# A GpSimd power ahead of all other work, and ten cosine products and eight key sums on VectorE in a hybrid encoder trunk

## The chip, the cores and the metric

The kernel runs on one core of one Trainium2 chip. The metric is the device time of one execution in microseconds (us), the median of several runs. TensorE (PE in the profile) multiplies matrices, VectorE (DVE) and ScalarE (ACT) work element by element, GpSimd (POOL) does a little arithmetic and starts some of the transfers, and SyncE (SP) starts the others.

## The reference

The kernel computes two layers of an encoder on 512 positions of 1024 features. Of each layer this is what matters here:

```python
xn = rms_norm(x, ln1[l])
z = xn @ w_in[l]
a_q, a_i, a_ff, a_fb, a_g, b_u, b_v, c_q, c_k, c_v, gz = split(z)
o_a = hgrn2_bidirectional(a_q, a_i, a_ff, a_fb, lower[l])   # branch A: 4 heads
y_a = rms_norm(o_a, a_norm[l]) * silu(a_g)
y_b = spatial_gating(gelu(b_u), gelu(b_v), w_s[l], b_s[l])  # branch B
qh, kh = partial_rope(c_q, pos), partial_rope(c_k, pos)     # branch C: t1*cos - t2*sin, t2*cos + t1*sin
y_c = window_attention(qh, kh, c_v, sink[l])
merged = (sigmoid(gz_0) * (y_a @ w_br[l, 0]) + sigmoid(gz_1) * (y_b @ w_br[l, 1])
          + sigmoid(gz_2) * (y_c @ w_br[l, 2]))
x = x + merged @ w_out[l]
x = x + square(relu(rms_norm(x, ln2[l]) @ w_up[l])) @ w_down[l]
```

Branch A is a gated linear recurrence in both directions. For one chunk, `attn = einsum(q_t, k_s, exp(b_t - b_s))` over all s up to t. The diagonal of it, where t equals s, has no decay: it is q times the key, and with two directions it is q times the sum of the forward and the backward key.

## The kernel before

**Products.** Every float32 product is three TensorE products of rounded parts: high times high, low times high, high times low (L200 to L202 with positions as the moving side, L242 to L244 for the other orientation). Weights come in pieces of 128x1024 through SP's queue. ACT rounds a piece to its high part `wh` (L195), and DVE subtracts it from the piece to get the low part `wl` (L196).

**Stages of a layer.** First the input is normalized and the wide projections for the values of A, the second half of B and the gates run as seven products instead of eight (L393 to L419 are their sums and products). Then come the branches, described next; then the branch outputs are projected (`yC`, `yA`, with tiles from L242 to L244), turned (`mT`, L1023), put through the output projection `wo`, and then through the MLP. The reciprocal square root of a norm is a power -0.5 on POOL (`rstd_c`, L262; and L818 for branch B). The first of them waits for DVE's L260, and PE's `bc` (L269) spreads its result over the columns.

**Branch A, one head** (`a_head`, L541 on). `ex` holds four rows of running log-decays. Seven levels L = 1, 2, 4 ... 64 follow each other. In each, ACT takes two exponentials of `ex` (`qt`, L552, and `kt`, L555), DVE multiplies `qt` by `q` (L553), PE forms 64-wide blocks `at` (L539), DVE or ACT puts them in place (L543 is the DVE one), and DVE adds across blocks in `ex` for the next level (two L580). At the first level the two keys are also exponentiated into `key` (L560), POOL adds them to `dg` (L562), and PE multiplies the sum by `q` for the diagonal. After the last level, `kd` (ACT, L592) is turned on PE (`kT`, L595), copied by ACT (L597), and multiplied with the values (`stp`, L600), once for each direction. The `q` and `f` of each head are projections of their own; DVE scales them as they leave PSUM (L685 for `q`, L693 for the gate inputs `z` from `f`).

**Branch C.** The key projection `ck` and the four query projections `cq` are rotated by `rot` (L865 to L871): DVE shuffles partitions (L867) and multiplies by the sine (L868), POOL multiplies the unshuffled tile by the cosine (L869), and DVE adds the two (L870). The rotated queries are split into parts (L898 on DVE), and the scores (`sc`, L914 and L915), turned probabilities (`pT`, L943) and outputs (`po`, L948) follow in blocks of 128 positions.

**Order.** The program is written with loops over heads, levels and blocks. A list scheduler with a simulated timeline, with priorities raised or lowered by helpers such as `hp()`, sets the order of the instructions on each engine when the kernel is built. So a change in what one engine is given can move the instructions of all. The order is fixed on each engine at run time, and semaphores tie the engines together. PSUM has eight banks in four pairs, and `q`, `f`, `ck`, `cq` and `gz` share one pair (`m`): a third product in a row waits until DVE or ACT has emptied the first. Tiles of the pool tag `a` (three buffers) hold `qt`, `kt`, `kd`, `qd` and `dg`.

Of the kernel before, what the change touches and what calls it, by code (L numbers as in the profile page):

```python
# [10 lines left out]
ALU = mybir.AluOpType  # L11
# [18 lines left out]
def ap_of(t, off, dims):  # L30
    return bass.AP(tensor=t.tensor, offset=t.offset + off, ap=[t.ap[0]] + dims)
# [28 lines left out]
def trunk(tc, xT, xt, ws, vec, fnb, bsb, snk, wst, rope, cmask, amask, ident, out):  # L60
    nc = tc.nc
# [30 lines left out]
    def nm(s):  # L92
        ctr[0] += 1
        return f"{s}_{ctr[0]}"

    def T(tag, name, dt=F32):
        where = part[HOME[tag]] if tag in HOME else sb
        return where.tile([P, S], dt, tag=tag, bufs=SLOTS[tag], name=nm(name))
# [8 lines left out]
    def Z2(name):  # L107
        return part["br"].tile([P, 2, S], F32, tag="z2", bufs=NZ, name=nm(name))

    def SM(tag, w):  # L110
        return pad.tile([P, w], F32, tag="sm_" + tag, bufs=4 if tag == "lb" else NSM, name=nm(tag))
# [4 lines left out]
    def PT(tag, name):  # L116
        return ps.tile([P, S], F32, tag="p_" + tag, bufs=BANKS[tag], name=nm(name))
# [31 lines left out]
    onep_t = cst.tile([P, 1], F32, name="onep_t")  # L149
    nc.vector.memset(onep_t, 1.0)  # L150

    mhalf_t = cst.tile([P, 4], F32, name="mhalf_t")
    nc.vector.memset(mhalf_t, -0.5)

    pad_t = pad.tile([P, 16], F32, name="pad_t")
    nc.vector.memset(pad_t, 0.0)

    nc.scalar.activation(pad_t[:, 1:2], pad_t[:, 0:1], AF.Square)

    def ln_ap(which, l, kt):  # L160
        c = {"ln1": 0, "ln2": 16, "fn": 32}[which] + (l * 8 if which != "fn" else 0) + kt
        return vec_t[:, c:c + 1]

    def anorm_ap(l):
        return vec_t[:, 40 + l:41 + l]
# [361 lines left out]
    def a_head(l, h, ex, q, vt):  # L527
        H = P // 2
        at = part["br"].tile([P, 4, P], F32, tag="at", bufs=1, name=nm("at"))
        own = part["br"].tile([P, 4, H], F32, tag="own", bufs=1, name=nm("own"))  # L530

        def attn(kk, qq, other=False):

            pt = PT("a", "at")
            for st in range(4):
                for h_ in range(2):
                    k0 = st * P + h_ * H
                    q0 = st * P + (1 - h_ if other else h_) * H
                    nc.tensor.matmul(pt[h_ * H:(h_ + 1) * H, st * H:(st + 1) * H], kk[:, k0:k0 + H], qq[:, q0:q0 + H], start=True, stop=True, skip_group_check=True)  # L539
            return pt[:, 0:4 * H].rearrange("p (a b) -> p a b", a=4)  # L540

        def put(pt, mi):
            nc.vector.copy_predicated(own, ap_of(amask_t, mi * H, [[0, 4], [1, H]]), pt)  # L543

        X, R, Y, PP = 0, S, 2 * S, 3 * S
        for li, L in enumerate(LEVELS):
            nb = 256 // L
            shp = "p (b h i) -> p b h i"
            e_k = ap_of(ex, 0, [[2 * L, nb], [2 * S + L, 2], [1, L]])
            e_q = ap_of(ex, S, [[2 * L, nb], [2 * S + L, 2], [1, L]])  # L550
            qt = T("a", "qt")
            nc.scalar.activation(qt.rearrange(shp, b=nb, h=2), e_q, AF.Exp)  # L552
            nc.vector.tensor_tensor(qt, qt, q, ALU.mult)  # L553
            kt_ = T("a", "kt")
            nc.scalar.activation(kt_.rearrange(shp, b=nb, h=2), e_k, AF.Exp)  # L555
            if L == 1:
                pt = attn(kt_, qt)
                nc.scalar.copy(own, pt)
                key = Z2("key")
                nc.scalar.activation(key, ap_of(ex, 0, [[2 * S, 2], [1, S]]), AF.Exp)  # L560
                dg = T("a", "dg")
                nc.gpsimd.tensor_tensor(dg, key[:, 0], key[:, 1], ALU.add)  # L562
                pt = attn(dg, q)
                put(pt, 0)
            elif L < H:
                put(attn(kt_, qt), li)
            else:
                pt = attn(kt_, qt, True)
                for h_ in range(2):
                    r = slice(h_ * H, (h_ + 1) * H)  # L570
                    nc.scalar.copy(at[r, :, (1 - h_) * H:(2 - h_) * H], pt[r])
                    nc.scalar.copy(at[r, :, h_ * H:(h_ + 1) * H], own[r])

            d = [[2 * L, nb], [1, L]]
            z = [[2 * L, nb], [0, L]]
            for o_, ostep, i_, istep in ((X, PP + L - X, PP + 2 * L - 1, -L), (Y + L, R - Y - L, R, L)):
                o_ap = ap_of(ex, o_, [[ostep, 2]] + d)
                nc.vector.tensor_tensor(o_ap, o_ap, ap_of(ex, i_, [[istep, 2]] + z), ALU.add)  # L580

        W3 = 3 * P
        dec = SM("ms", 4)
        nc.scalar.activation(dec[:, 0:2], ap_of(ex, PP + 2 * P - 1, [[P, 2]]), AF.Exp)
        nc.scalar.activation(dec[:, 2:4], ap_of(ex, R + P, [[P, 2]]), AF.Exp)
        sts, qds = [], []
        for dr, (ko, qo) in enumerate(((0, P), (P, 0))):

            kd = T("a", "kd")[:, 0:W3]
            nc.scalar.activation(kd, ex[:, 2 * dr, ko:ko + W3], AF.Exp)  # L592
            pt = PT("a", "kT")
            for i in range(3):
                nc.tensor.transpose(pt[:, i * P:(i + 1) * P], kd[:, i * P:(i + 1) * P], id_t)  # L595
            kT = part["br"].tile([P, W3], F32, tag="kT", bufs=1, name=nm("kT"))
            nc.scalar.copy(kT, pt[:, 0:W3])  # L597
            ps_ = PT("a", "stp")
            for i in range(3):
                nc.tensor.matmul(ps_[:, i * P:(i + 1) * P], kT[:, i * P:(i + 1) * P], vt[ko // P + i][:, h * P:(h + 1) * P], start=True, stop=True)  # L600
            st_ = part["br"].tile([P, 3, P], F32, tag="st", bufs=2, name=nm("st"))
            order = (0, 1, 2) if dr == 0 else (2, 1, 0)
            nc.vector.tensor_copy(st_[:, order[0]], ps_[:, order[0] * P:(order[0] + 1) * P])
            for a_, b_ in zip(order, order[1:]):

                c = b_ - 1 if dr == 0 else 2 + b_
                nc.vector.scalar_tensor_tensor(st_[:, b_], st_[:, a_], dec[:, c:c + 1], ps_[:, b_ * P:(b_ + 1) * P], ALU.mult, ALU.add)
            qd = T("a", "qd")[:, 0:W3]
            nc.scalar.activation(qd, ex[:, 3 - 2 * dr, qo:qo + W3], AF.Exp)
            nc.vector.tensor_tensor(qd, qd, q[:, qo:qo + W3], ALU.mult)  # L610
            sts.append(st_)
            qds.append(qd)

        po = PT("a", "av")
        for tt in range(4):
            c = slice(tt * P, (tt + 1) * P)
            parts = [(at[:, tt], vt[tt][:, h * P:(h + 1) * P])]
            if tt > 0:
                parts.append((qds[0][:, (tt - 1) * P:tt * P], sts[0][:, tt - 1]))
            if tt < 3:  # L620
                parts.append((qds[1][:, c], sts[1][:, tt]))
            for i, (w_, m_) in enumerate(parts):
                nc.tensor.matmul(po[:, c], w_, m_, start=i == 0, stop=i == len(parts) - 1)
        sq = T("a", "asq")
        ss = SM("ss", 4)
        for tt in range(4):
            c = slice(tt * P, (tt + 1) * P)
            nc.scalar.activation(sq[:, c], po[:, c], AF.Square, accum_out=ss[:, tt:tt + 1])
        rc = rstd_c(ss, P)
        o = T("a", "ao")  # L630
        nc.vector.tensor_tensor(o.rearrange("p (a b) -> p a b", a=4), po.rearrange("p (a b) -> p a b", a=4), ap_of(rc, 0, [[1, 4], [0, P]]), ALU.mult)
        pt = PT("a", "oT")
        for tt in range(4):
            c = slice(tt * P, (tt + 1) * P)
            nc.tensor.transpose(pt[:, c], o[:, c], id_t)
        on = T("l", "on")
        nc.scalar.activation(on, pt, AF.Copy, scale=anorm_ap(l))
        return on
# [40 lines left out]
    for l in range(DEPTH):  # L679
# [114 lines left out]
        wst_t, bsb_t, cos_t, sin_t = (T("l", n) for n in ("wst", "bsb", "cos", "sin"))  # L794
# [26 lines left out]
        for g in range(4):  # L821
            pt = PT("s", "mx")
# [42 lines left out]
        def rot(z):  # L865
            sh = T("g", "sh")
            nc.vector.stream_shuffle(sh, z, list(range(8, 16)) + list(range(8)) + list(range(16, 32)))  # L867
            nc.vector.tensor_tensor(sh, sh, sin_t, ALU.mult)  # L868
            nc.gpsimd.tensor_tensor(z, z, cos_t, ALU.mult)  # L869
            nc.vector.tensor_tensor(z, z, sh, ALU.add)  # L870
            return z  # L871

# [14 lines left out]
        pt = PT("c", "vT")  # L887
# [222 lines left out]
        for qd in range(4):  # L1110
# [6 lines left out]
            for f in range(8):  # L1117
                pt = proj(n2.xs, f'up{qd}', l, "up", qd, f, bank="s" if f % 4 > 1 else "m")
# [152 lines left out]
```

## Time and profile before

| what | value |
|---|---|
| median of 3 runs | 1727.49 us (1726.69 to 1728.23) |
| the profiled execution's own time | 1725.17 us |
| span of its profile | 1723.3 us |
| mean granted TensorE clock | 0.993 |
| PE busy | 1677.8 us, 97% |
| DVE busy | 1288.6 us, 75% |
| ACT busy | 1009.1 us, 59% |
| POOL busy | 150.9 us, 9% |

The span runs from the first to the last instruction in the trace; the execution's own time is 1.9 us longer. A row of the timeline gives the start, the duration, the engine, the line, the operation with what it writes and reads, and in brackets how long the engine sat idle before it and what released it. A row of the waits says which instruction of an engine waited, for whom, how long in total, how often, and the longest time. A row of windows gives for a stretch the busy time of PE, weight loads, DVE, ACT and POOL, then the granted clock of TensorE. Matmuls are pipelined, so that their start-to-start time, not their duration, is what one costs.

### The profile page before, as it was taken

How to read it: one execution, taken by the hardware profiler on the slowest of the kernel's cores; microseconds unless marked ns; L12 is line 12 of the kernel's file. 1: busy time of each engine (PE TensorE's matmuls, PEld its weight loads, DVE VectorE, ACT ScalarE, POOL GpSimd, SP SyncE). 2: the span in 40 equal slices, each digit the busy share in tenths (PEclk: the TensorE clock that was granted, in tenths of full speed). 3: DMA queues.
4: the chain of work that ended last, by engine and by line, in shares of the span. 5: the costliest groups of instructions: out<-in, count | busy, mean ns of one | idle time of the engine just before them, and what ended most of it. 6: DMA issues, size and time to landing. Idle time of an engine off the chain costs nothing.

```text
span 1723.3 us, 23007 instructions
## 1 busy us (share of the span) xinstructions
PE 1677.8 (97%) x8536; PEld 1380.8 (80%) x8536; DVE 1288.6 (75%) x2031; ACT 1009.1 (59%) x1691; POOL 150.9 (9%) x215
## 2 busy tenths in 40 slices
PE   6999999999999999999999999999999999999997
PEld 5888877888878888888878887788878788888886
DVE  7996986678465858687889869876875667676867
ACT  6665577677425555454666665877782355545464
POOL 1021210100220000000010202001004100000001
PEclk9999999999999999999999999999999999999999
DMA  8243221222465232332332332222315453232311
GB/s 317 76 147 109 75 95 63 98 87 86 141 230 191 86 123 95 114 103 95 132 123 98 135 103 86 92 69 97 104 56 220 178 182 106 98 110 86 123 62 49
DMA packets 58143, 199.84 MB, mean 116 GB/s; under 512 B 7888, under 2 KB 8144, under 8 KB 58032
## 3 DMA queue, kind: packets, MB, share of 16 engines
q1 hardware_dynamic: 44496, 154.46, 26.2%
q0 software_dynamic: 13248, 43.40, 6.7%
q8 instruction: 67, 1.10, 0.3%
q10 hardware_dynamic: 288, 0.52, 0.1%
q14 instruction: 44, 0.36, 0.1%
HBM read 177.38 MB, written 20.97 MB: 115 GB/s over the span
## 4 chain that ended last, share of the span: by engine, by line
PE 81%; DVE 8%; ACT 5%; issue 4%; DMA 2%; POOL 1%; SPq 0%; POOLq 0%; DVEq 0%; ACTq 0%
PE up L200 7%; PE up L201 7%; PE up L202 7%; PE dA L406 3%; PE dA L407 3%; PE dA L408 3%; PE po L948 2%; PE wo L243 2%; PE wo L242 2%; PE dC L407 2%; PE dC L406 2%; PE dC L408 2%; PE wo L244 2%; PE gz L202 1%; PE gz L201 1%
## 5 line engine op out<-in xcount | busy, mean ns | idle before, releaser
L195 ACT CAST wh<-wq 128x1024 fp32r<-128x1024 f32 x196 | 206.2, 1052 | 211.6 <-PE dA L407 50.8
L196 DVE TENSOR_TENSOR wl<-wr,wh 128x1024 fp32r<-128x1024 f32 x171 | 208.9, 1222 | 154.5 <-ACT wh L195 153.8
L195 ACT CAST wh<-wr 128x1024 fp32r<-128x1024 f32 x171 | 179.2, 1048 | 230.9 <-PE up L201 88.3
L196 DVE TENSOR_TENSOR wl<-wq,wh 128x1024 fp32r<-128x1024 f32 x196 | 239.2, 1222 | 87.5 <-ACT wh L195 86.2
L201 PE MATMUL up<-xl,wh 128*128 128x512 f32 x512 | 199.3, 390 | 0.0
L202 PE MATMUL up<-xh,wl 128*128 128x512 f32 x512 | 199.3, 390 | 0.0
L200 PE MATMUL up<-xh,wh 128*128 128x512 f32 x512 | 198.8, 390 | 0.0
L202 PEld LDWEIGHTS up<-xh,wl 128*128 128x128 f32 x512 | 96.2, 188 | 20.1
L200 PEld LDWEIGHTS up<-xh,wh 128*128 128x128 f32 x512 | 96.2, 188 | 19.8
L201 PEld LDWEIGHTS up<-xl,wh 128*128 128x128 f32 x512 | 96.2, 188 | 19.7
L406 PE MATMUL dA<-wh,sh 128*128 128x512 f32 x256 | 99.8, 390 | 0.0
L407 PE MATMUL dA<-wh,sh 128*128 128x512 f32 x256 | 99.7, 390 | 0.0
L408 PE MATMUL dA<-wl,sh 128*128 128x512 f32 x256 | 92.7, 390 | 0.0
L580 DVE TENSOR_TENSOR ex<-ex 128x512 f32<-128x512 f32 x112 | 74.9, 685 | 4.8 <-ACT kt L555 4.5
L552 ACT ACTIVATE qt<-ex 128x512 f32<-128x512 f32 x56 | 37.8, 675 | 50.1 <-DVE ex L580 39.0
L262 POOL TENSOR_TENSOR rs<-ms,mhalf_t 128x4 f32<-128x4 f32 (+2 forms) x15 | 18.5, 1232 | 497.6 <-DVE ms L260 493.4
L408 PEld LDWEIGHTS dA<-wl,sh 128*128 128x128 f32 x256 | 48.1, 188 | 10.0
L406 PEld LDWEIGHTS dA<-wh,sh 128*128 128x128 f32 x256 | 48.1, 188 | 9.9
L407 PEld LDWEIGHTS dA<-wh,sh 128*128 128x128 f32 x256 | 48.1, 188 | 9.9
L200 PE MATMUL gz<-xh,wh 128*128 128x512 f32 x128 | 51.6, 403 | 0.0
L202 PE MATMUL gz<-xh,wl 128*128 128x512 f32 x128 | 51.4, 402 | 0.0
L201 PE MATMUL gz<-xl,wh 128*128 128x512 f32 x128 | 51.1, 399 | 0.0
(405 smaller groups left out, 4352.2 us busy)
## 6 DMA issues: line engine op xcount, KB each, us to landing
wr<-in_ws_dram SPq DMA_DIRECT2D x171, 512.0 KB, 3.3
wq<-in_ws_dram SPq DMA_DIRECT2D x112, 512.0 KB, 4.2
thd<-zt POOLq DMA_DIRECT2D x32, 256.0 KB, 2.6
th<-thd POOLq DMA_DIRECT2D x32, 256.0 KB, 4.4
mgd<-mg POOLq DMA_DIRECT2D x16, 256.0 KB, 2.4
mcd<-th POOLq DMA_DIRECT2D x16, 256.0 KB, 2.6
mC<-mcd POOLq DMA_DIRECT2D x16, 256.0 KB, 6.2
mB<-mgd POOLq DMA_DIRECT2D x16, 256.0 KB, 5.9
```

Source lines behind the costliest of these rows:

```text
L195: nc.scalar.copy(hi, raw)
L196: nc.vector.tensor_tensor(lo, raw, hi.bitcast(F32), ALU.subtract)
L200: nc.tensor.matmul(pt, whi, xhi, start=first, stop=False)
L201: nc.tensor.matmul(pt, whi, xlo, start=False, stop=False)
L202: nc.tensor.matmul(pt, wlo, xhi, start=False, stop=last)
L242: nc.tensor.matmul(pts[t], xh, hi[:, c], start=k == 0, stop=False)
L243: nc.tensor.matmul(pts[t], xl, hi[:, c], start=False, stop=False)
L406: nc.tensor.matmul(pt, xh[:, t], hi[:, c], start=start and k == 0, stop=False, skip_group_check=True)
L407: nc.tensor.matmul(pt, xl[:, t], hi[:, c], start=False, stop=False, skip_group_check=True)
L408: nc.tensor.matmul(pt, xh[:, t], lo[:, c], start=False, stop=k == 3, skip_group_check=True)
L552: nc.scalar.activation(qt.rearrange(shp, b=nb, h=2), e_q, AF.Exp)
L580: nc.vector.tensor_tensor(o_ap, o_ap, ap_of(ex, i_, [[istep, 2]] + z), ALU.add)
```

## The change

Three things change. A power of one element per partition, of no use to any result, is put on POOL directly after the constants are set. The sum of the two keys of branch A is made by DVE, in place in the first key, instead of by POOL in a tile of its own. And the cosine product of `rot` is made by DVE instead of POOL. The first occurs once, the second 8 times (4 heads, 2 layers), the third 10 times (5 tiles, 2 layers).

```diff
@@ -156,6 +156,7 @@
     nc.vector.memset(pad_t, 0.0)
 
     nc.scalar.activation(pad_t[:, 1:2], pad_t[:, 0:1], AF.Square)
+    nc.gpsimd.tensor_tensor(pad_t[:, 2:3], onep_t, mhalf_t[:, 0:1], ALU.pow)
@@ -558,9 +559,8 @@
                 key = Z2("key")
                 nc.scalar.activation(key, ap_of(ex, 0, [[2 * S, 2], [1, S]]), AF.Exp)
-                dg = T("a", "dg")
-                nc.gpsimd.tensor_tensor(dg, key[:, 0], key[:, 1], ALU.add)
-                pt = attn(dg, q)
+                nc.vector.tensor_tensor(key[:, 0], key[:, 0], key[:, 1], ALU.add)
+                pt = attn(key[:, 0], q)
                 put(pt, 0)
@@ -866,7 +866,7 @@
             nc.vector.tensor_tensor(sh, sh, sin_t, ALU.mult)
-            nc.gpsimd.tensor_tensor(z, z, cos_t, ALU.mult)
+            nc.vector.tensor_tensor(z, z, cos_t, ALU.mult)
             nc.vector.tensor_tensor(z, z, sh, ALU.add)
```

What stands on lines 159 to 560 before is one line further down after; from the key sum (L562) on, and so in `rot`, the numbers are the same.

The order of the instructions is the same on all engines for the first 180 us, and in the MLP. In the two stretches with the branches the scheduler arrives at another order on PE, DVE and ACT.

The first place is on DVE in layer 1, where the last tile `cq` is rotated beside the later levels of head 0, and where `z`, the gate input of head 1, is taken from its bank `f` (L693). Before:

```order
L898 TENSOR_TENSOR q_2113_10047<-cq_9350,q_2113_10047 64x512
L580 TENSOR_TENSOR ex_8809<-ex_8809 128x2x8x32 x2
L870 TENSOR_TENSOR cq_9383<-cq_9383,sh_10204 128x512
L898 TENSOR_TENSOR q_2114_10048<-cq_9350,q_2114_10048 64x512
L693 TENSOR_TENSOR z_2001_9557<-f_2005_9564,rb_7932 128x512
L196 TENSOR_TENSOR wl_10369<-wr_10366,wh_10368 128x1024
L543 COPY_PREDICATED own_8859<-amask_t,at_8964 128x256
L553 TENSOR_TENSOR qt_8976<-qt_8976,q_8856 128x512
L580 TENSOR_TENSOR ex_8809<-ex_8809 128x2x4x64 x2
L898 TENSOR_TENSOR q_2161_10209<-cq_9383,q_2161_10209 64x512
L898 TENSOR_TENSOR q_2162_10210<-cq_9383,q_2162_10210 64x512
L693 TENSOR_TENSOR z_2001_9557<-f_2009_9596,rb_7932 128x512
```

And now (L197 is the low part of a weight piece, L554 the product of `qt` and `q`, L544 the placing of `at`):

```order
L898 TENSOR_TENSOR q_2060_9881<-cq_9313,q_2060_9881 64x512
L898 TENSOR_TENSOR q_2107_10042<-cq_9346,q_2107_10042 64x512
L693 TENSOR_TENSOR z_1996_9553<-f_2000_9560,rb_7929 128x512
L868 TENSOR_TENSOR sh_10199<-sh_10199,sin_8736 128x512
L869 TENSOR_TENSOR cq_9379<-cq_9379,cos_8735 128x512
L197 TENSOR_TENSOR wl_10364<-wr_10361,wh_10363 128x1024
L554 TENSOR_TENSOR qt_8955<-qt_8955,q_8853 128x512
L898 TENSOR_TENSOR q_2108_10043<-cq_9346,q_2108_10043 64x512
L544 COPY_PREDICATED own_8856<-amask_t,at_8943 128x256
L580 TENSOR_TENSOR ex_8806<-ex_8806 128x2x8x32 x2
L870 TENSOR_TENSOR cq_9379<-cq_9379,sh_10199 128x512
L693 TENSOR_TENSOR z_1996_9553<-f_2004_9592,rb_7929 128x512
```

The first L693 stood behind four L898, the scans of the level of 32 (`128x2x8x32 x2`) and the addition of the rotation; it now stands ahead of the sine and cosine products of the last tile and ahead of those scans. The second L693 stood behind the scans of the last level (`4x64`), which now come after it.

The second place is on PE in layer 0, where head 0's first turned tile `kT` meets the projections `f` and `q` of head 1. Before:

```order
L201 MATMUL f_456_2154<-xl_172,wh_2150 128x512
L202 MATMUL f_456_2154<-xh_171,wl_2151 128x512
L200 MATMUL f_456_2154<-xh_175,wh_2150 128x512
L595 MATMUL kT_1525<-id_t,kd_1523 128x128 x3
L201 MATMUL f_456_2154<-xl_176,wh_2150 128x512
L202 MATMUL f_456_2154<-xh_175,wl_2151 128x512
L914 MATMUL sc_1981<-k_398_1948,q_405_1972 128x256
L915 MATMUL sc_1981<-kl_1950,q_405_1972 128x256
```

And now:

```order
L203 MATMUL f_455_2154<-xh_176,wl_2151 128x512
L914 MATMUL sc_1981<-k_397_1948,q_404_1972 128x256
L915 MATMUL sc_1981<-kl_1950,q_404_1972 128x256
L914 MATMUL sc_1986<-k_398_1949,q_405_1973 128x256
L915 MATMUL sc_1986<-kl_1951,q_405_1973 128x256
L540 MATMUL at_1505<-qt_1500,kt_1503 64x64 x8
L595 MATMUL kT_1525<-id_t,kd_1523 128x128 x3
L201 MATMUL q_2195<-xh_148,wh_2191 128x512
```

The turn `kT` stood two products ahead of the end of `f`; it now stands behind all of `f`, four scores of branch C and the last level's `at`.

The third place is on PE in layer 1, at the end of head 3, where projections of branch C (`yC`) stand between the small products. Before:

```order
L539 MATMUL at_11208<-qt_11203,kt_11206 64x64 x8
L943 MATMUL pT_10533<-id_t,sc_10338 128x128 x2
L595 MATMUL kT_11228<-id_t,kd_11226 128x128 x3
L948 MATMUL po_10537<-pT_10528,cvt_9407 128x256 x2
L600 MATMUL stp_11234<-vt_7799,kT_11232 128x128
L600 MATMUL stp_11234<-vt_7801,kT_11232 128x128
L600 MATMUL stp_11234<-vt_8014,kT_11232 128x128
L595 MATMUL kT_11247<-id_t,kd_11245 128x128 x3
L242 MATMUL yC_11618<-wh_11654,yh_11606 128x512
L242 MATMUL yC_11619<-wh_11654,yh_11606 128x512
```

And now:

```order
L595 MATMUL kT_11221<-id_t,kd_11219 128x128 x3
L943 MATMUL pT_10528<-id_t,sc_10333 128x128 x2
L600 MATMUL stp_11227<-vt_7796,kT_11225 128x128
L600 MATMUL stp_11227<-vt_7798,kT_11225 128x128
L600 MATMUL stp_11227<-vt_8011,kT_11225 128x128
L595 MATMUL kT_11240<-id_t,kd_11238 128x128 x3
L948 MATMUL po_10532<-pT_10523,cvt_9403 128x256 x2
L600 MATMUL stp_11246<-vt_7798,kT_11244 128x128
L600 MATMUL stp_11246<-vt_8011,kT_11244 128x128
L600 MATMUL stp_11246<-vt_8013,kT_11244 128x128
L623 MATMUL av_11257<-vt_7796,at_11079 128x128
L243 MATMUL yC_11611<-wh_11647,yh_11599 128x512
```

Between the second `kT` and its `stp` stood twelve products of `yC`; there is now one `po` there, and `yC` follows behind `av`.

On POOL the new power stands first, ahead of four loads of constants. The order of SP's queue is the same.

## The prediction

> **What bounds the kernel now.** I read the busy times of the page first, then the waits of PE, then the windows around the largest of them, and last the timeline of DVE and POOL in those windows.
>
> ```profile
> PE 1677.8 (97%) x8536; PEld 1380.8 (80%) x8536; DVE 1288.6 (75%) x2031; ACT 1009.1 (59%) x1691; POOL 150.9 (9%) x215
> ```
>
> PE is the bound: 1723.3 - 1677.8 = 45.5 us is all that it is not busy. An edit on DVE and POOL can win only from PE's waits and from matmuls at a lowered clock, and it can lose by new waits. These are the largest waits of PE that DVE or POOL could have a hand in (line waiting, releaser, total, times, longest):
>
> ```profile
> PE bc L269 <- POOL rs L262: 5.2, 1, 5.2
> PE q L200 <- DVE z L693: 3.5, 1, 3.5
> PE kT L595 <- ACT kd L592: 2.6, 2, 2.0
> PE at L539 <- DVE qt L553: 2.3, 1, 2.3
> PE stp L600 <- ACT kT L597: 1.6, 2, 1.3
> ```
>
> The windows tell what surrounds them (stretch, length, busy of PE, weight loads, DVE, ACT, POOL, then the granted clock):
>
> ```profile
> 180.00:230.00 50.00, 47.88 (x316) 37.84 (x315) 48.74 (x74) 25.93 (x43) 12.04 (x8) 1.00 0.23 74
> 266.00:278.00 12.00, 8.26 (x41) 6.83 (x42) 9.01 (x20) 10.54 (x22) 0.56 (x1) 0.72 0.32 110
> 300.00:360.00 60.00, 60.00 (x402) 49.69 (x402) 38.56 (x83) 42.28 (x84) 4.49 (x6) 1.00 0.25 88
> 1030.00:1090.00 60.00, 56.53 (x335) 45.00 (x333) 58.43 (x90) 36.87 (x53) 11.61 (x9) 0.97 0.21 72
> 1284.00:1300.00 16.00, 12.84 (x107) 10.26 (x104) 10.96 (x22) 12.05 (x31) 1.17 (x3) 1.00 0.12 38
> ```
>
> In the two stretches in which branch C is rotated beside head 0 of branch A (180 to 230 and 1030 to 1090) DVE has 97% of the time booked, and PE falls idle because of it. Later, beside the other heads (300 to 360), DVE has 38.56 of 60 and PE does not wait at all. So an operation of DVE counts in the rotation stretches and not elsewhere.
>
> **DVE beside a POOL product.** This is DVE's and POOL's timeline in layer 1 (start, duration), and then the groups of DVE's multiplications by line, first those of the stretch 180 to 230, then those of 1030 to 1090 (busy time and mean ns of one):
>
> ```profile
> 1052.92 2.11 POOL L869 TENSOR_TENSOR cq<-cq,cos 128x512 f32<-128x512 f32 x1 [6.72 <-DVE sh L867]
> 1053.80 1.78 DVE L553 TENSOR_TENSOR qt<-qt,q 128x512 f32<-128x512 f32 x1
> 1055.50 0.68 DVE L868 TENSOR_TENSOR sh<-sh,sin 128x512 f32<-128x512 f32 x1
> 1056.10 0.43 DVE L543 COPY_PREDICATED own<-amask_t,at 128x256 f32<-128x256 uint8 x1
> ```
>
> ```profile
> L553 DVE TENSOR_TENSOR qt<-qt,q 128x512 f32<-128x512 f32 x7 | 6.6, 946 | 0.0
> L868 DVE TENSOR_TENSOR sh<-sh,sin 128x512 f32<-128x512 f32 x5 | 6.4, 1275 | 0.0
> L870 DVE TENSOR_TENSOR cq<-cq,sh 128x512 f32<-128x512 f32 x4 | 2.7, 686 | 0.8 <-POOL cq L869 0.8
> L553 DVE TENSOR_TENSOR qt<-qt,q 128x512 f32<-128x512 f32 x7 | 5.8, 835 | 0.0
> L868 DVE TENSOR_TENSOR sh<-sh,sin 128x512 f32<-128x512 f32 x5 | 5.4, 1088 | 0.0
> L898 DVE TENSOR_TENSOR q<-cq,q 64x512 fp32r<-64x512 f32 x8 | 6.5, 809 | 0.2
> ```
>
> A 128x512 product of DVE takes 0.68 us, and the next one starts 0.60 after it (1055.50 to 1056.10). The one that begins inside a POOL product takes 1.78, 1.10 more: POOL's cosine product costs DVE time, though it is there to save DVE work. Made by DVE itself it should cost the 0.60 of any product of this size.
>
> **The change, part by part.**
>
> *The sums on DVE.* In layer 0's rotation stretch, the seven L553 take 6.6 where 7 x 0.68 = 4.8 would do, the five L868 6.4 for 3.4, and one addition waits 0.8 for POOL: 1.8 + 3.0 + 0.8 = 5.6 us of stalls. Added are five cosine products and one key sum, 6 x 0.60 = 3.6. DVE is 2.0 us shorter there. In layer 1 the stalls are 1.0 (L553), 2.0 (L868) and 1.0 (L898, 6.5 for 8 x 0.68), in sum 4.0 against the same 3.6: 0.4 shorter. The six key sums of heads 1 to 3 add 0.60 each to a DVE that has a third of its time free (300 to 360), with PE's own matmuls as cover; were that cover gone, they would cost 3.6 us together. I take 0.
>
> *Layer 1's rotation.* This is where the scheduler's new order weighs more than the microseconds above.
>
> ```profile
> 1080.01 1.29 DVE L580 TENSOR_TENSOR ex<-ex 128x512 f32<-128x512 f32 x2
> 1082.65 0.69 DVE L693 TENSOR_TENSOR z<-f,rb 128x512 f32<-128x512 f32 x1
> 1085.32 1.29 DVE L580 TENSOR_TENSOR ex<-ex 128x512 f32<-128x512 f32 x2
> ...
> 1083.40 0.50 PE L200 MATMUL q<-xh,wh 128*128 128x512 f32 x1 [3.47 <-DVE z L693]
> 1086.71 0.63 PE L200 MATMUL q<-xh,wh 128*128 128x512 f32 x1
> 1087.13 0.63 PE L201 MATMUL q<-xl,wh 128*128 128x512 f32 x1
> 1087.84 0.39 PE L200 MATMUL q<-xh,wh 128*128 128x512 f32 x1
> 1088.07 0.39 PE L201 MATMUL q<-xl,wh 128*128 128x512 f32 x1
> ```
>
> PE waits 3.47 us for z to leave its bank, since z stands behind a pair of scans and five operations of branch C. Then nine matmuls start 0.42 apart (1086.71 to 1087.13) where 0.23 is usual (1087.84 to 1088.07): 9 x 0.20 = 1.8 more. In the new order z stands ahead of a pair of scans (1.2), the level's product and placing (0.6 + 0.3), the rotation's sine product and addition (1.2) and one split (0.7): 4.0 us. Of the additions four cosine products and the key sum stand before it, 3.0, for the 4.0 of stalls that go, and 1.0 more if the key sum's own stall ahead of the stretch is counted. That puts z at 1077 to 1078, before PE asks for it (1083.40 - 3.47 = 1079.93). So 3.47 + 1.8 = 5.3 us go. What is late next: head 0's last scans, at 1085.32 before, now have the sine, cosine and a level's work ahead of them and come at about 1091. The first kd follows 3 us later and meets `kT` at the place where PE is at 1093.7: 0.7 to 1 us of new wait. Net: -4.3 (between -5.3 and 0).
>
> *Layer 0's rotation.*
>
> ```profile
> 228.29 0.55 PE L595 MATMUL kT<-id_t,kd 128*128 128x128 f32 x3 [1.97 <-ACT kd L592]
> 241.41 0.94 PE L600 MATMUL stp<-vt,kT 128*128 128x128 f32 x6 [1.27 <-ACT kT L597]
> ```
>
> The last scans come 2 us of stalls earlier, and `kT` stands behind two products, four scores and one `at` that were behind it: about 1.5 us later on PE. Both waits should close, the second because its kd is earlier by the same: -1.97 - 1.27 = -3.2 (between -3.2 and 0).
>
> *Head 1's first levels, layer 0.*
>
> ```profile
> 268.15 0.90 PE L539 MATMUL at<-qt,kt 128*64 128x64 f32 x16 [2.30 <-DVE qt L553]
> 270.63 0.90 PE L943 MATMUL pT<-id_t,sc 128*128 128x128 f32 x3 [1.59 <-ACT yc L950]
> 268.26 1.28 ACT L491 ACT_TABLE_LOAD   x1
> ```
>
> ACT holds PE up here with table loads of 1.28 us, 2.30 + 1.59, and the clock falls to 0.72 of full speed in the window, which is another 1.8 as above: 5.7 in all. The loads stay, but with the new order PE comes to this place with other matmuls ahead of it. I take -2.0, a third of it, between -5.7 and 0.
>
> *Ends of the heads.* At the end of head 3 in layer 1, PE is busy 12.84 of 16 us. Twelve `yC` products that stood between `kT` and `stp` (12 x 0.23 = 2.8 us of cover) are gone from there, and in all about 20 matmuls less, of `yC` and `ag`, stand among the head's last levels (20 x 0.23 = 4.6). In layer 0 this place has been without them already and waits about as long in sum as layer 1 does. I take +2.0 for both layers, between 0 and +6.
>
> *The power ahead of all.*
>
> ```profile
> 37.49 4.88 POOL L262 TENSOR_TENSOR rs<-ms,mhalf_t 128x4 f32<-128x4 f32 x1 [12.53 <-DVE ms L260]
> 37.64 2.36 DVE L196 TENSOR_TENSOR wl<-wq,wh 128x1024 fp32r<-128x1024 f32 x2
> 40.25 1.23 DVE L196 TENSOR_TENSOR wl<-wq,wh 128x1024 fp32r<-128x1024 f32 x1
> 42.43 2.08 PE L269 MATMUL bc<-id_t,rs 128*128 128x128 f32 x8 [5.18 <-POOL rs L262]
> ...
> 119.93 4.65 POOL L818 TENSOR_TENSOR lr<-lr,mhalf_t 128x1 f32<-128x1 f32 x1
> 122.94 1.22 DVE L419 TENSOR_TENSOR wq<-wq,wq 128x1024 f32<-128x1024 f32 x1
> ```
>
> The first power of the kernel takes 4.88 us and PE waits 5.18 for it, the largest wait that the change aims at. It runs beside a closed row of two-input DVE operations and ends 0.89 after the last of them (37.49 + 4.88 = 42.37; 40.25 + 1.23 = 41.48). A power at 119.93, the fifth of the kernel, is as long, 4.65, with nothing left to be made ready; it too runs beside such a row and ends 0.42 after it (124.58 against 124.16). So the length is DVE's doing, and a power made earlier changes nothing of it: 0. It costs nothing either, since POOL has been idle for 12.53 us when that power comes. Bounds: from -4.5 (the first rival) to +0.5 for an operation that ends a little later.
>
> [...]
>
> The sum: -4.3 - 3.2 - 2.0 + 2.0 + 0 = -7.5. Against the profiled execution's own 1725.17 us that is 1717.7. That execution lies 2.3 below the median of the runs, so for a median I say 1727.5 - 7.5 = **1720.0 us**.
>
> **The rivals.**
>
> *The first power does pay for being first.* Then rs is ready at about 38.6, and PE's `bc` could follow. The tile `xs` that comes next on PE is held by DVE's row until 41.48 + 0.7, so PE is at its 44.16 point some 2.4 us earlier, and with a wait below 2 us the slowed matmuls after it go as well, up to 4.5 in all. Another -3.5: 1716.5. For it: it is the first use. Against it: the row at 119.93, and the exact end of DVE's row. [...] Chance 0.14.
>
> *The gain is given back along the heads.* PE is one chain of matmuls with small products of the heads in between. If z comes early but head 0's levels come late by as much, layer 1 wins nothing, the place at 268 keeps its waits, and the ends take +2: -3.2 + 2.0 = -1.2, or 1726.3, no change that can be told. A difference under 0.2% (3.5 us) is within what a measurement of this kernel can tell. For it: the last scans do come 5 us later in layer 1's order. Chance 0.16.
>
> *DVE pays.* If the stretched rows are only in part POOL's doing, or the operations that would meet the POOL product wait for something else anyway, DVE pays 6 x 0.60 = 3.6 us in each rotation stretch where it is 97% booked and PE waits on it, and none of the waits above closes: +7.2, or 1734.7. It decides from the point where less than 3.6 of stalls per layer goes. For it: in layer 1 the stalls of 4.0 are near that point. Against it: the plain and the stretched durations differ exactly where a POOL product runs. Chance 0.20.
>
> **How the numbers follow.** The forecast has 0.50. Faster by over 0.2%: 0.50 + 0.14 = 0.64; within: 0.16; slower: 0.20. The range goes down to 1710: the forecast with the place at 268 at its full -5.7 and the ends at 0, 1714.3, and the first rival's gain of up to 4.5. It goes up to 1731: the sum with layer 1 and 268 at nothing and the ends at +6 is +2.8 or 1730.3. The third rival's full price is left outside.
>
> **What would show it.** Right: no L553 or L868 over 0.8 us in the rotation stretches; PE's wait for z (L693) gone or under 1 us; `kT` of layer 0 without its 1.97; the first power of `rstd_c` still near 4.9. Wrong: the first power near 1 us and `bc` waiting under 2 (first rival); PE waiting over 3 us for kd in layer 1, or at head 3's `stp` over 4 (second); a DVE in the rotation stretches still at 97% and a longer wait for z (third).

## The result, and the profile after

The kernel after takes 1714.13 us in the median of 6 runs (1712.88 to 1715.80), the kernel before 1726.70 (1723.96 to 1728.23): a ratio of 0.9928, with a 95% interval of 0.9916 to 0.9939. That is 12.6 us faster. The forecast was 7.5 us faster, and 1720.0 us with a range of 1710 to 1731. The profiled execution of the kernel after has a span of 1712.9 us, 10.4 less than before.

The busy times of the page, and five of the waits of PE, after (line waiting, releaser, total, times, longest; L201 and L270 are L200 and L269 of before):

```profile
PE 1675.5 (98%) x8536; PEld 1379.8 (81%) x8536; DVE 1285.7 (75%) x2049; ACT 1009.5 (59%) x1691; POOL 122.0 (7%) x198
```

```profile
PE bc L270 <- POOL rs L263: 5.2, 1, 5.2
PE mT L1023 <- DVE mB L1028: 3.8, 6, 1.1
PE stp L600 <- ACT kT L597: 3.0, 2, 2.7
PE kT L595 <- ACT kd L592: 1.5, 1, 1.5
PE at L540 <- ACT kt L556: 1.3, 2, 0.7
```

PE's wait for z, 3.5 us before, is not in the list any more, and the wait of `at` for `qt` is gone too. The wait for the first norm's power is as it was. DVE has 18 operations more and is busy 2.9 us less.

The windows of the rotation stretches of both layers, of the place where head 1 begins in layer 0, and of the end of head 3 in layer 0 (stretch, length, busy of PE, weight loads, DVE, ACT, POOL, then the granted clock):

```profile
180.00:230.00 50.00, 50.00 (x328) 40.14 (x327) 49.60 (x86) 28.42 (x47) 0.00 (x0) 1.00 0.25 80
266.00:278.00 12.00, 11.37 (x79) 9.08 (x78) 9.00 (x21) 10.10 (x18) 0.55 (x1) 1.00 0.19 67
1023.00:1083.00 60.00, 60.00 (x360) 48.62 (x359) 58.04 (x98) 38.73 (x54) 1.39 (x3) 1.00 0.25 81
422.00:440.00 18.00, 13.30 (x87) 11.05 (x88) 9.15 (x24) 11.74 (x32) 0.00 (x0) 0.81 0.09 30
```

PE is busy 50.00 of 50 and 60.00 of 60 where it was 47.88 and 56.53 (layer 1 runs 6.8 us earlier now, so its window is moved by 7). At 266 to 278 it does 79 instructions instead of 41. The fourth row is the other side: PE stands still for 4.7 of 18 us there, with the clock at 0.81; at the same place before, 429 to 447, it was 1.1 us and 1.00.

DVE's multiplications by `q` (L554) and by the sine (L868) over the whole kernel (shortest, median, longest in ns), and DVE around head 0's late levels in layer 1:

```profile
L554 DVE TENSOR_TENSOR qt<-qt,q x56: 662/686/694, 180.8 to 1274.9; 128x512 f32<-128x512 f32 x56
L868 DVE TENSOR_TENSOR sh<-sh,sin x10: 673/680/692, 188.9 to 1070.6; 128x512 f32<-128x512 f32 x10
```

```profile
1069.99 0.69 DVE L693 TENSOR_TENSOR z<-f,rb 128x512 f32<-128x512 f32 x1
1070.60 0.68 DVE L868 TENSOR_TENSOR sh<-sh,sin 128x512 f32<-128x512 f32 x1
1071.19 0.68 DVE L869 TENSOR_TENSOR cq<-cq,cos 128x512 f32<-128x512 f32 x1
...
1083.33 1.28 DVE L580 TENSOR_TENSOR ex<-ex 128x512 f32<-128x512 f32 x2
```

None of these products is stretched any longer. In the time scale of before, 6.77 us later, z leaves its bank at 1076.8 and the last scans come at 1090.1; the prediction had 1077 to 1078 and 1091.

### The profile page after: what moved, and what is told of

It is laid out like the page before. It is cut to its first block, busy times and chain, and to the rows that moved or that the text cites. A ratio compares the mean times of both kernels' runs of the same rounds, so it can differ in the third digit from the quotient of the medians.

```text
span 1712.9 us, 22985 instructions
## 1 busy us (share of the span) xinstructions
PE 1675.5 (98%) x8536; PEld 1379.8 (81%) x8536; DVE 1285.7 (75%) x2049; ACT 1009.5 (59%) x1691; POOL 122.0 (7%) x198
## 4 chain that ended last, share of the span: by engine, by line
PE 86%; ACT 5%; DVE 4%; DMA 2%; issue 1%; POOL 1%; SPq 0%; POOLq 0%; ACTq 0%; DVEq 0%
PE up L202 7%; PE up L201 7%; PE up L203 7%; PE dA L408 3%; PE dA L407 3%; PE dA L409 3%; PE po L948 2%; PE gA L407 2%; PE wo L244 2%; PE at L540 2%; PE dC L408 2%; PE dC L407 2%; PE dC L409 2%; PE gA L409 2%; PE gA L408 2%; PE wo L243 2%
## 5 line engine op out<-in xcount | busy, mean ns | idle before, releaser
L197 DVE TENSOR_TENSOR wl<-wr,wh 128x1024 fp32r<-128x1024 f32 x171 | 208.8, 1221 | 154.2 <-ACT wh L196 153.3
L197 DVE TENSOR_TENSOR wl<-wq,wh 128x1024 fp32r<-128x1024 f32 x196 | 239.0, 1221 | 89.0 <-ACT wh L196 87.8
L201 PE MATMUL up<-xh,wh 128*128 128x512 f32 x512 | 198.6, 389 | 0.0
L201 PEld LDWEIGHTS up<-xh,wh 128*128 128x128 f32 x512 | 96.1, 188 | 20.1
L554 DVE TENSOR_TENSOR qt<-qt,q 128x512 f32<-128x512 f32 x56 | 38.4, 686 | 18.9 <-ACT qt L553 18.5
L553 ACT ACTIVATE qt<-ex 128x512 f32<-128x512 f32 x56 | 37.7, 674 | 24.5 <-DVE ex L580 19.4
L251 ACT CAST sh<-sf 128x512 fp32r<-128x512 f32 x64 | 39.6, 619 | 19.4 <-DVE sf L372 17.5
L201 PE MATMUL gz<-xh,wh 128*128 128x512 f32 x128 | 50.7, 396 | 0.0
```

The costliest lines, as they stand in the source:

```text
L197: nc.vector.tensor_tensor(lo, raw, hi.bitcast(F32), ALU.subtract)
L201: nc.tensor.matmul(pt, whi, xhi, start=first, stop=False)
L251: nc.scalar.copy(hi, src)
```

## The experiments

**Each part alone.** Three kernels make one of the three changes to the kernel before.

The power ahead of all other work, alone:

```diff
     nc.scalar.activation(pad_t[:, 1:2], pad_t[:, 0:1], AF.Square)
+    nc.gpsimd.tensor_tensor(pad_t[:, 2:3], onep_t, mhalf_t[:, 0:1], ALU.pow)
```

> The power of one element ahead of all other work, alone; nothing else and no order differs from before. Theory (the first norm's power is held by DVE's row of two-input operations): that power stays at 4.9 us, PE's bc still waits 5.2, and the time is that of before within 1.5 us. Rival (the first power pays for being first): the power takes about 1 us, bc waits under 2, 2.4 to 4.5 us faster.

Measured: 1725.31 us against 1727.0, a ratio of 0.9993 (0.9983 to 1.0004): nothing that can be told from zero. POOL's timeline in it:

```profile
1.05 0.54 POOL L159 TENSOR_TENSOR pad_t<-onep_t,mhalf_t 128x1 f32<-128x1 f32 x1 [0.61 <-DVE pad_t L156]
36.66 4.89 POOL L263 TENSOR_TENSOR rs<-ms,mhalf_t 128x4 f32<-128x4 f32 x1 [12.52 <-DVE ms L261]
```

The first power of all takes 0.54 us, no more than a later one of its size (the trace of before has 0.54 to 0.58 for five of its ten powers of 128x1). So there was nothing to be made ready, and the power that PE waits for stays at 4.89.

The cosine products on DVE, alone:

```diff
-            nc.gpsimd.tensor_tensor(z, z, cos_t, ALU.mult)
+            nc.vector.tensor_tensor(z, z, cos_t, ALU.mult)
```

> The ten cosine products on DVE, key sums left on POOL. Port theory (DVE loses time to each POOL product it meets, and PE waits on DVE in the rotation stretches): the stalls of the cosine products go (about 4 us per layer) against 3.0 added, L868 falls to 0.68 everywhere, and with the waits for z and kd going most of the gain is there: 6 to 11 us faster. Rival (the scheduler's new order does it, whatever the port): the gain is not tied to the stalls, anything between 0 and 12, with PE's waits elsewhere than in the rotation stretches deciding.

Measured: 1715.01 us, a ratio of 0.9933 (0.9918 to 0.9948). By the ratios that is 11.6 us, where all three changes together win 12.4, and a little more than the upper end of the expectation. The sine product takes 0.67 to 0.69 us everywhere, as the port theory has it. (The name is mine: the runs show the time that DVE loses beside a POOL product, 1.10 us for the L553 at 1053.80 of before, and no run shows a port as the cause.) But the rival's 0 to 12 holds 11.6 as well, so this run alone does not tell the two apart. The windows of its rotation stretches, in which PE is busy 49.99 of 50 and 58.57 of 60 us:

```profile
180.00:230.00 50.00, 49.99 (x326) 39.90 (x325) 49.59 (x85) 29.65 (x49) 5.43 (x3) 1.00 0.26 85
1023.00:1083.00 60.00, 58.57 (x363) 46.95 (x361) 58.38 (x100) 39.88 (x54) 3.09 (x4) 1.00 0.26 85
```

The key sums on DVE, alone:

```diff
-                dg = T("a", "dg")
-                nc.gpsimd.tensor_tensor(dg, key[:, 0], key[:, 1], ALU.add)
-                pt = attn(dg, q)
+                nc.vector.tensor_tensor(key[:, 0], key[:, 0], key[:, 1], ALU.add)
+                pt = attn(key[:, 0], q)
```

> The eight key sums on DVE, cosine products left on POOL. Port theory: only one stalled L553 (1.10) and one L520 (0.99) go, 8 x 0.60 come; L868 keeps its 1.3 in the middle, and PE keeps its waits in the rotation stretches: within 3 us of before. Rival (the new order does it): some 4 to 12 faster, as with the cosine products.

Measured: 1723.55 us, a ratio of 0.9984 (0.9974 to 0.9993): 2.8 us faster (1.2 to 4.5 by the interval), mostly in the port theory's bounds of 3 us; only its upper part touches the rival's 4 to 12. Its waits of PE, and the sine product (L867 in this kernel):

```profile
PE kT L594 <- ACT kd L591: 3.8, 3, 2.6
PE q L200 <- DVE z L692: 2.3, 1, 2.3
PE at L539 <- DVE qt L553: 1.8, 2, 0.9
```

```profile
L867 DVE TENSOR_TENSOR sh<-sh,sin x10: 679/1450/1790, 190.6 to 1075.6; 128x512 f32<-128x512 f32 x10
```

DVE's order is another one here as well, about as far from that of before as in the kernel with the cosine products; yet the sine product stays at 1.45 in the middle, and PE keeps its waits for kd and z. So this other order, with the cosine products left on POOL, does not win the 12 us. What the order of the kernel after would win with them on POOL was not run.

**The POOL products put back, with nothing else moved.** The kernel after, with ten POOL products of the same size that nobody reads. Every other instruction stands in the order of the kernel after, on all engines.

```diff
             nc.vector.tensor_tensor(sh, sh, sin_t, ALU.mult)
+            nc.gpsimd.tensor_tensor(T("jk", "sp"), sh, cos_t, ALU.mult)
             nc.vector.tensor_tensor(z, z, cos_t, ALU.mult)
```

> The kernel after, with ten POOL products of 128x512 put back that nobody uses (sine-multiplied tile by cosine, into a spare buffer), started where the rotation starts them; the order of all other instructions on all engines is that of the kernel after. Port theory: each stalls a DVE operation by 0.77 to 1.10, four to five us per layer, DVE in the rotation stretches is over-full, and PE waits there again: 4 to 9 us slower than the kernel after (1718 to 1723). Rival (the order does it): 1714 as the kernel after, within 1.5.

Measured: 1724.04 us, 0.9984 of before (0.9974 to 0.9994), so by the two ratios 9.7 us above the kernel after, somewhat more than the upper end of the expectation. Its timeline at the first of them, and then its groups of DVE, three of the stretch 180 to 232 and two of 1025 to 1088 (count, busy time, mean ns of one):

```profile
188.94 1.66 POOL L869 TENSOR_TENSOR sp<-sh,cos 128x512 f32<-128x512 f32 x1 [24.78 <-DVE sh L868]
189.37 1.78 DVE L580 TENSOR_TENSOR ex<-ex 128x512 f32<-128x512 f32 x1
```

```profile
L580 DVE TENSOR_TENSOR ex<-ex 128x512 f32<-128x512 f32 x14 | 11.2, 815 | 0.0
L197 DVE TENSOR_TENSOR wl<-wr,wh 128x1024 fp32r<-128x1024 f32 x7 | 9.5, 1354 | 0.0
L899 DVE TENSOR_TENSOR q<-cq,q 64x512 fp32r<-64x512 f32 x6 | 5.1, 846 | 0.2
...
L197 DVE TENSOR_TENSOR wl<-wr,wh 128x1024 fp32r<-128x1024 f32 x9 | 13.3, 1477 | 0.0
L554 DVE TENSOR_TENSOR qt<-qt,q 128x512 f32<-128x512 f32 x7 | 7.0, 996 | 0.0
```

The stalls now fall on other operations: the scan that starts 0.43 us into the POOL product takes 1.78 and ends 0.55 after it (191.15 against 190.60). In the kernel after, the same groups take 9.3 for the 14 scans, 1.21 for a weight split, 4.1 for the six L898 and 4.8 for the seven products by `q`. The excess is 1.9 + 1.0 + 1.0 = 3.9 us in layer 0 and 13.3 - 9 x 1.21 = 2.4 and 2.2, together 4.6, in layer 1: 8.5 us. The span is 1721.2, which is 8.3 more than the kernel after. So DVE's stalls reach the end nearly in full. PE's waits in this kernel say where:

```profile
PE q L201 <- DVE z L693: 5.0, 2, 3.1
PE at L540 <- ACT kt L556: 1.3, 2, 0.7
PE gz L201 <- DVE z L693: 1.0, 1, 1.0
```

The wait for z is back, 3.1 in layer 0 and the rest in layer 1, and layer 1's first `kT` now waits 1.04 for kd. The place at 268, on the other hand, still waits only 0.63 for `at`, with the POOL products present: that gain does not depend on them.

**The first norm's power.** In the kernel after, three weight splits that ran beside the power on DVE are made to come after it, by a copy of four elements of its result into the tile that each split then overwrites:

```diff
+    gate = []
...
         nc.scalar.copy(hi, raw)
+        rc = gate.pop() if gate else None
+        if rc is not None:
+            nc.vector.tensor_copy(lo[:, 0:4], rc)
         nc.vector.tensor_tensor(lo, raw, hi.bitcast(F32), ALU.subtract)
...
             boost[0] = True
+            gate.extend([n1.rc] * 3 + [None] * 2)
```

> The kernel after, in which the three weight splits of DVE that ran beside the first norm's power are made to wait for it: a copy of four elements of rs into each split's tile stands ahead of it on DVE, and the split overwrites them. Only two small DVE operations (0.42 each) are left beside the power. Theory (DVE's row of two-input operations holds the power): it takes 1.0 to 1.8 us instead of 4.89, bc waits 1 to 2 instead of 5.2, and the splits come about as late as the power did, so that PE gets back 1 to 3 us: 1711 to 1713. Rival (the first four-element power, or the first norm, is slow by itself): the power stays near 4.9, DVE waits for it, and the time is 1714 to 1718.

Measured: 1710.74 us, 0.9908 of before (0.9891 to 0.9924). This is the fastest of all, a little below the 1711 to 1713 expected: 3.4 us below the kernel after by the medians, while the intervals of the two ratios just overlap (0.9916 to 0.9939 there) and the spans of the two profiled executions differ by 1.8. Its timeline:

```profile
38.48 1.15 POOL L267 TENSOR_TENSOR rs<-ms,mhalf_t 128x4 f32<-128x4 f32 x1 [12.76 <-DVE ms L265]
38.75 0.42 DVE L379 SCALAR_TENSOR_TENSOR sf<-x,sf 128x256 f32<-128x256 f32 x1
39.66 0.31 DVE L200 CAST wl<-rs 128x4 fp32r<-128x4 f32 x3 [0.48 <-POOL rs L267]
39.67 1.16 PE L274 MATMUL bc<-id_t,rs 128*128 128x128 f32 x8 [1.72 <-POOL rs L267]
39.94 3.49 DVE L201 TENSOR_TENSOR wl<-wq,wh 128x1024 fp32r<-128x1024 f32 x3
43.49 0.73 PE L413 MATMUL tA<-wl,xs 128*128 128x512 f32 x2 [1.72 <-DVE wl L201]
```

The same power takes 1.15 us (the eleven later ones of this size in the kernel before take 1.03 to 1.04) and ends 0.46 after the last DVE operation beside it (39.63 against 39.17). DVE idles 0.48 for it. PE's wait falls from 5.2 to 1.72, its eight `bc` products take 1.16 instead of 2.08 (the granted clock is 1.00 from 39 to 42 us, where the kernel after has 0.50 from 42 to 46), and 1.72 comes back as a wait for the first late split. Neither wait of 1.72 lowers the clock (1.00 from 36 to 50), and in the kernel before the wait of 1.97 at 228 did not either (1.00 from 228 to 234), while after the kernel after's wait of 2.67 at 432 it was 0.50 (432.4 to 436). Of the 5.2 us and the slow matmuls behind them 1.8 (by the spans) to 3.4 us (by the medians) are won.

## Why the prediction was right, and where its sizes were off

**The sums on DVE: right in the stalls, open in their share of the gain.** No L554, L868 or L869 is above 0.70 us, and the added operations, L562 and L869, take 0.68 like any other of this size. The prediction's sums had DVE 2.4 us shorter in the two stretches together; over the whole kernel it is busy 2.9 us less. The spare products show that such stalls reach the end: with the order unchanged, the span falls 8.3 us when they go. They do not show how the 10.4 us divide between the stalls and the new order, because in that kernel DVE makes its ten cosine products too, some 10 x 0.60 = 6 us, beside the POOL ones. If that work reaches the end as the stalls do, the exchange of stalls for products is worth 8.3 - 6.0 = 2.3 us, and the other 8 come with the new order; that is an estimate. A kernel in the new order with the cosine products on POOL would decide it, and was not run.

**Layer 1's rotation: the mechanism right, -4.3 was too small.** The wait of 3.47 and its slow matmuls went (5.3), but the new wait of 0.7 to 1 us for kd did not come: the list of PE's waits after has a single one for kd, and that is in layer 0. PE came to `kT` at 1087.64, which is 1094.4 in the scale of before and 0.7 later than the 1093.7 I had, and kd was there. With the spare products the wait is there, with 1.04 us.

**Layer 0's rotation: right.** Both waits, 1.97 and 1.27, are gone, as the -3.2 had it. Whether the earlier scans or the later `kT` closed them is not shown: with the spare products they stay away too, but there PE is held 3.1 us for z ahead of them.

**The place at 268: the term that was most mis-sized.** I took a third of 5.7 us. The waits there fell from 3.89 to the 0.63 of one `at`, and the clock from 266 to 278 went from 0.72 to 1.00: about 5.1 of the 5.7. I had left the term at a third, because the table loads of ACT stay, and the third was a choice, not worked out. Four loads of 1.28 us do stand there still (262.78 to 270.03), but PE now has other matmuls to do meanwhile, 79 in the 12 us. The gain stays with the spare products present, so it does not hang on the stalls, which leaves the new order; the kernel with the key sums alone, in its own order, still waits 1.91 and 1.76 there.

**Ends of the heads: +2.0 was too small for layer 0.** This is PE's timeline in the kernel after, at the end of head 3 there:

```profile
428.76 0.55 PE L595 MATMUL kT<-id_t,kd 128*128 128x128 f32 x3 [1.52 <-ACT kd L592]
432.40 1.65 PE L600 MATMUL stp<-vt,kT 128*128 128x128 f32 x6 [2.67 <-ACT kT L597]
```

The window of this place before, and its `stp` then:

```profile
429.00:447.00 18.00, 16.90 (x117) 13.58 (x116) 10.49 (x22) 11.57 (x29) 0.68 (x2) 1.00 0.11 37
440.19 0.94 PE L600 MATMUL stp<-vt,kT 128*128 128x128 f32 x6 [0.34 <-ACT kT L597]
```

Now the two waits alone are 4.2 us, and the clock falls to 0.81 in their window. The prediction had taken this place to wait about as long as layer 1's before, and that was a misreading: it waited 1.1 us in all, layer 1's 3.2 (16 - 12.84). So it had more to lose than I thought. Layer 1's end, for which I had feared more, did not change by more than a few tenths. A version without the new wait was not tried.

**The power: right at 0**, and for the reason given. The row of DVE operations holds it: the gated kernel takes away the row and the power takes 1.15 us instead of 4.89, while with a power made earlier it stays at 4.89.

**The rivals.** The first use of the power is excluded by its 0.54 us. The gain was not given back along the heads, though part of it was at layer 0's end. DVE did not pay: with the stalls gone it is even a little fuller (49.60 of 50 against 48.74) and gets more done, 86 operations in the 50 us instead of 74. I had named a DVE still at 97% together with a longer wait for z as the sign of this rival; the first half came and the second did not, so a full DVE by itself was no sign.

In all, the forecast's -7.5 became -10.4 between the two profiled executions and -12.6 between the medians. The profiled execution of before, at 1725.17, lies 1.5 below its median, and that of after, at 1714.73, 0.6 above its own; that is the difference. The place at 268 (by 3.1 us) and layer 1's rotation (by 1.0) were taken too small, the ends of the heads too favourable (by 1 to 1.5 us and the lowered clock). Two things had no term: PE's 2.1 us wait at `wo` in layer 0 is gone, and the waits at `mT` for `mB` went from 2.3 in sum to 3.8. That these two nearly cancel is luck, and which edit moved them is open. The range of 1710 to 1731 would have held no change as well, so the signs, which came as named, say more for the mechanism than the time does. The parts do not add either: by their ratios 1.2, 11.6 and 2.8 us make 15.6, not 12.4, each with an order of its own.

## What to carry to other kernels

An operation handed to a slow engine can still cost the busy engine time (here a cosine product takes 1.63 to 2.18 us on POOL in the kernel before, 0.67 to 0.69 on DVE in the kernel after): compare the durations of the busy engine's operations beside the helper's and away from them, and set the excess against the price of doing the work itself. Here ten POOL products cost DVE 8.5 us in stretches where it had 97% of its time booked, against some 6 us for making them itself, and nearly all of the 8.5 reached the end. An edit that also gives the program another order needs a run with the order held; the run here held it and showed the cost of the stalls, but not what the order alone is worth. When an engine's short operation is slow, look at what its neighbour runs at the same time before making it ready in advance: holding back three operations won 1.8 to 3.4 us, the early power nothing that can be told from zero.

## What the runs showed of the hardware that was not expected

In layer 0 of the kernel with the spare products, each of the five POOL products of 128x512 (1.58 to 1.66 us) held up one DVE operation until it was done: two scans and an L899 ended 0.55 us after it (1.45 to 1.78 instead of 0.68), two weight splits of 128x1024 1.07 and 1.09 (1.70 and 1.72 instead of 1.21). An L544 and an L685 that began inside two of these products took no longer than elsewhere (0.45 and 0.68). POOL's small power did the opposite beside an unbroken row of DVE operations. It ended 0.89 and 0.42 us after the last of the row in the kernel before and 0.46 in the gated one, whether the row went on for 0.7 us beside it (1.15 in all, gated) or for 4.0 (4.88, before).

Size does not decide which of the two happens. In the kernel with the cosine products alone, POOL's first key sum meets an unbroken row of DVE operations and takes 4.39 us, where the others of this kernel take 1.27 to 1.32, and one 1.96; that is some 3 us more, and then it held up a weight split, which ended 1.08 after it (1.72):

```profile
180.16 4.39 POOL L562 TENSOR_TENSOR dg<-key 128x512 f32<-128x512 f32 x1 [15.76 <-ACT key L560]
183.91 1.72 DVE L196 TENSOR_TENSOR wl<-wr,wh 128x1024 fp32r<-128x1024 f32 x1
```

In the kernel before, the same key sum, beside a row as closed, took 1.38 and held up DVE's L553 (1.78). So the same operation on the same engines did both; why POOL sometimes gets in and sometimes waits was not tried.
